# A decoder layer's first feed-forward: accumulating transfers for the residual, and a new order around its first product pairs

## The chip, the cores and the metric

The kernel runs on one core of one Trainium2 chip. The metric is device time in microseconds (us) of one launch; the figure compared is the median of several runs. The core has five engines with queues of their own: TensorE (PE, matrix products; PEld is its weight loading), VectorE (DVE), ScalarE (ACT), GpSimd (POOL) and SyncE (SP, which here only issues transfers). Each works through its instructions in order and waits on semaphores. ACT and POOL issue transfers too, in line with their other instructions.

## The reference

One decoder layer on x, 1024 tokens by 1024 channels, float32: a half-weighted feed-forward, a mixer (stick-breaking attention beside a Mamba-2 scan), a cross-attention to 256 memory tokens, and a second half-weighted feed-forward. Each part is normalised before and after. Only the first feed-forward bears on the change:

```python
f = swiglu(rmsnorm(h, ffn1_pre_g[l]), ffn1_w_gu[l], ffn1_w_down[l])
h = h + 0.5 * rmsnorm(f, ffn1_post_g[l])
m = hybrid_mixer(rmsnorm(h, mix_pre_g[l]), ...)
# swiglu(h): g, u = split(h @ w_gu); (silu(g) * u) @ w_down      inner width 2816 = 22 x 128
```

## The kernel before

Activations lie with channels on the 128 partitions and tokens along the free axis, in two halves `hh` of 512 tokens; a tile is 128 x 512. Eight tiles `d` make a half. Every operand of a product is kept as a high part (`XH`, `whi`), rounded to the format that PE takes, and a low part (`XL`, `wlo`), what rounding lost. `mm3` (L281) multiplies high by high, high by low and low by high, so a 128 x 128 block of weights against one tile is three matmuls of 512 columns. `split` (L259) makes the parts: the high one on ACT (L261), the low one on DVE (L263). Where a line of the profile reads `xl<-braw,xh` at L263, it is such a low part.

`up_phase` (L556) makes the 22 blocks `f` of gate and up. The first three (`first_seven` is 3 here) go plainly, block by block and half by half: `gate` and `up`. The other 19 go through `seven(f)` (L804), a fast scheme that makes gate and up for both halves with seven products in place of eight, each of 4 x 3 = 12 matmuls. The products' right operands are the four quarters `B11`, `B12`, `B21`, `B22` of the normalised input and three sets of sums `S`; the quarter `B12` is turned into a difference in place (`differ`, L727) and split by `last` (L717), one tile at a time, from 2.5 us after the first `seven` begins. The left operands are sums and differences of the weights' halves, made in `pieces` (L746): a 128x512 POOL instruction (L757) and a `split`. `blocks`, `ahead` and `block` hand them out in the order of the products and make up to four in advance. `prepare_all` (L234) uses the same stretch to load later weights (31 blocks, 62 steps), split them and store the parts in DRAM; a step borrows the tiles `acc0`, `acc1`, `rpost`, `dg`, `bh`, `bl`.

The down projection (`down1` L952, `down7` L992) is again seven products `m`, over 11 pairs of blocks. It needs sums of the activations of four quarters, `xs`: pairs of blocks from 4 up make them while they are at hand (`pair_sums`, L633); for the first two pairs they are loaded again, summed on DVE (L616) and stored by `act_sums` (L597), which `seven(f)` starts for f = 4 and 5. Operands of the down projection are loaded, combined (L1031) and split by `fetch`, five or more ahead.

After the products come `squares` (the sum of squares) and `post` (L380). It scales a result tile `F` by gain and norm (`apply`, L401), adds the residual tile that `resid` (L370) loaded into an `XL` tile on POOL's queue (L405), stores the new `h` (L410, POOL's queue), makes the high part for the mixer (L412, ACT) and, later, the low part (`low`, L417, DVE) and the sum of squares (`presum`, L363). For half 0 this lies beside the last products of the down projection, for half 1 beside the mixer's first projections (`ssd`).

What sets the order: PE's instructions keep the order of the program. `self.clock` adds up a planned cost of each matmul (0.422 ns a column, 216 ns for 512). Work put on `self.later` with a planned time enters the program when the clock has reached it, and is pinned behind what its engine already has (`kp`). The rest is ordered by a scheduler from data dependencies; `urgent` raises an instruction's priority. All times such as 148000, 14000 or 2600 in the code are nanoseconds on that planned clock.

Of the kernel before, what the change touches and what calls it, by code (L numbers as in the profile page):

```python
# [47 lines left out]
class Kern:  # L48
# [189 lines left out]
    def prepare_all(self, sp):  # L238
        names = [("ssd", i) for i in [*range(6), *range(12, 26)]] + [("qkv", i) for i in range(QKV)]
        pairs = [  # L240
            ((self.fp, "acc0", None), (self.fp, "acc1", None)), ((self.fp, "rpost", None), (self.tp, "dg", None)),
            ((sp, "bh", None), (sp, "bl", None)),
        ]
        raw = [(sp, "braw", 2), (sp, "braw", 2), (self.xp, "xl0", KT + 1), (self.xp, "xl1", KT + 1)]
        n = 2 * len(names)
        self.prepare(names, raw, pairs, [148000 + 3900 * i for i in range(n)])

# [131 lines left out]

    def post(self, hh, gname, r2, gnext=None, out=None, step=None, spread=True, pins=(23000, 28000), accs=None, at=None, tail=None, hold=False):  # L380


        nc = self.nc
        t1, t2 = 2500, 6000
        if accs is None:
            accs = self.new_accs()
            for d in range(KT):
                self.sumsq(accs, d, self.F[hh][d])
# [9 lines left out]
        def apply(d):  # L398
# [4 lines left out]
                )  # L403
            )
            self.kp(nc.vector.tensor_tensor(out=F, in0=F, in1=self.XL[hh][d], op=ALU.add))  # L405
            if out is not None:
                nc.sync.dma_start(out=out[d], in_=F)
                return
            self.XL[hh][d] = self.xl(hh, F32R)
            self.kp(nc.gpsimd.dma_start(out=self.h[hh][d], in_=F))  # L410
# [19 lines left out]

        def rest(d):
            low(d)
            presum(d)
# [16 lines left out]
        for d in range(KT):  # L450
            t = t3 + step * d
            q.append((t, lambda d=d: apply(d)))
            if out is None:
                q.append((t + min(step, 2600) + 300, lambda d=d: rest(d)))
        if out is None:
            t += min(step, 2600)
            c2 = self.t(self.rp, [P, 4], F32, f"cpre{hh}", bufs=2)
# [98 lines left out]
    def up_phase(self, sp, sp2, wgu, gpre, act_d, bank, load, plain, sizes, rw=None, begin=None):  # L556
# [40 lines left out]
        def act_sums(j, t0):  # L597

            x = {}
            names = ("a11", "a21", "a12", "a22")  # L600
            late = 14000 if begin else 9000

# [22 lines left out]
            for i, (n, out, a, b, op) in enumerate((  # L625
# [4 lines left out]
                at(t0 + late + 1200 * i, combine, n, out, a, b, op)  # L630
                at(t0 + late + 3000 + 1200 * i, put, n)

# [113 lines left out]
        def pieces(f):  # L746
# [3 lines left out]
            G0, G1, U0, U1 = G[:, 0:4], G[:, 4:8], U[:, 0:4], U[:, 4:8]  # L750
            for a, b, op in (
                (G0, G1, ALU.add), (U1, None, None), (G0, U1, ALU.add), (U0, G0, ALU.subtract), (G0, None, None),
                (G1, U1, ALU.subtract), (U0, U1, ALU.add),
            ):
                if b is not None:
                    t = self.t(sp if begin else sp2, [P, 4, P], F32, "wc", bufs=NWC)
                    inst = nc.gpsimd.tensor_tensor(out=t, in0=a, in1=b, op=op)  # L757
                    if begin and f == first_seven and a is G0 and b is G1:
                        self.tc.keep_in_program_order(inst)
                    a = t  # L760
# [43 lines left out]
        def seven(f):  # L804


            t5, d = (self.t(self.tp, [P, H], F32, f"sq{i}") for i in range(2))
            if later_sums and (f in (4, 5) if begin else f > 6 and f % 2):
                act_sums(later_sums.pop(0), self.clock)
# [16 lines left out]
            with self.urgent():  # L826
                nc.vector.tensor_tensor(out=e, in0=e, in1=m6, op=ALU.add)
            product(a, B12, True)
            t1 = ft()
            with self.urgent():  # L830
                scaled(t1, a, 1)
            with self.urgent():
                nc.vector.tensor_tensor(out=e, in0=e, in1=a, op=ALU.add)
            product(c, S[5], True)
# [7 lines left out]
            with self.urgent():  # L842
                nc.vector.tensor_tensor(out=e, in0=e, in1=b, op=ALU.subtract)  # L843
            nc.gpsimd.tensor_tensor(out=t1, in0=t1, in1=e, op=ALU.mult)  # L844
            if f < 4:
# [106 lines left out]
    def down1(self, sp, wdn, act_d, xs_d, gpost, gnext):  # L952
# [5 lines left out]
        accs = []  # L958
# [9 lines left out]
        def finish(m, i):  # L968
            if m == 3:
                self.run_later(float("inf"))  # L970
                for d in range(4):
                    at(5000 + 4000 * d, squares, 0, d, "acc0")
                self.resid(0, 3500, 16000)
            elif m == 4:
# [1421 lines left out]
```

## Time and profile before

| | us |
|---|---|
| median of 3 runs | 2607.29 (2604.95 to 2607.7) |
| span of the profiled execution | 2606.7 |
| PE busy | 2578.2 (99%) |
| DVE busy | 1993.9 (76%) |
| ACT busy | 1289.7 (49%) |
| POOL busy | 577.9 (22%) |

The profiled execution's own time is its span, 2606.7 us from the first instruction to the last; nothing else is recorded around it, and it lies 0.6 us under the median of the runs. All times in a trace count from the span's start. The plain blocks run up to 79 us, the `seven` pairs from 80 to 449, the down projection from there to 666, and the mixer's first projections follow. A timeline row gives start, length, engine, line, operation, `output<-inputs`, and in brackets how long the engine was idle before it and who released it. The length of a matmul reaches past the start of the next one.

### The profile page before, as it was taken

Reading aid. Unit: us, or ns where it says so; the run is one execution under the profiler, and the core shown is the slowest. Engines: PE = TensorE matmul, PEld = TensorE weight load, DVE = VectorE, ACT = ScalarE, POOL = GpSimd, SP = SyncE. Lnnn points to the kernel's source line nnn. Section 1 sums busy time; section 2 is a strip of 40 time slices with the busy share of each in tenths; the row PEclk is TensorE's granted clock in tenths of the full one; section 3 lists DMA queues with packets and bytes.
Section 4 is the critical chain, followed back from the end, with each engine's and each line's share of the span. In section 5 each row is a group of like instructions: output and inputs, shape, how many; then the busy total and the mean of one; then the engine's idle time right before and its main releaser. Section 6 shows DMA issues by size and latency. Waiting matters only on the chain.

```text
span 2606.7 us, 36814 instructions
## 1 busy us (share of the span) xinstructions
PE 2578.2 (99%) x12850; PEld 2148.5 (82%) x12850; DVE 1993.9 (76%) x3044; ACT 1289.7 (49%) x2300; POOL 577.9 (22%) x669
## 2 busy tenths in 40 slices
PE   9999999999999999999999999999999999999999
PEld 7788888888777778888888898888878888888887
DVE  7978987779689884777777777876656888777767
ACT  7434444555356663555555554445554433334543
POOL 2655554001000001111111110101011655551000
PEclk9999999999999999999999999999999999999999
DMA  6468887655656516555555556547558453326554
GB/s 241 158 210 298 300 287 272 209 188 169 224 195 204 182 69 213 162 149 152 141 152 131 169 161 215 206 153 250 196 185 299 146 183 104 109 85 236 184 174 154
DMA packets 216042, 489.82 MB, mean 188 GB/s; under 512 B 26544, under 2 KB 35120, under 8 KB 215856
## 3 DMA queue, kind: packets, MB, share of 16 engines
q1 hardware_dynamic: 169232, 381.02, 44.6%
q0 software_dynamic: 22720, 62.93, 8.1%
q10 hardware_dynamic: 23904, 43.53, 4.5%
q8 instruction: 101, 1.65, 0.3%
q14 instruction: 85, 0.70, 0.1%
HBM read 327.46 MB, written 138.94 MB: 179 GB/s over the span
## 4 chain that ended last, share of the span: by engine, by line
PE 77%; issue 13%; DVE 5%; ACT 1%; DMA 1%; POOL 0%; DVEq 0%; ACTq 0%; POOLq 0%
PE mm L139 38%; PE dn L139 34%; PE z L139 2%; PE tr L142 2%; PE ms L139 1%; PE ms L142 1%; DVE nb L1770 1%; DVE wlo L263 0%; DVE acc L363 0%; DVE hl L263 0%; DVE atl L263 0%; DVE F L1053 0%; DVE xl L263 0%; DVE F L405 0%; DVE xl L417 0%
## 5 line engine op out<-in xcount | busy, mean ns | idle before, releaser
L139 PE MATMUL mm<-xh,whi 128*128 128x512 f32 x1320 | 520.3, 403 | 2.5 <-ACT xh L268 1.1
L139 PE MATMUL mm<-xh,wlo 128*128 128x512 f32 x1272 | 488.7, 391 | 0.0
L139 PE MATMUL mm<-xl,whi 128*128 128x512 f32 (+1 forms) x1252 | 486.9, 389 | 1.8 <-DVE xl L263 1.4
L139 PEld LDWEIGHTS mm<-xh,whi 128*128 128x128 f32 x1320 | 248.2, 188 | 44.6 <-issue 3.8
L139 PEld LDWEIGHTS mm<-xh,wlo 128*128 128x128 f32 x1272 | 238.8, 188 | 52.1 <-DVE wlo L263 0.4
L139 PEld LDWEIGHTS mm<-xl,whi 128*128 128x128 f32 x1252 | 236.1, 189 | 35.9 <-DVE xl L263 2.3
L1770 DVE TENSOR_TENSOR_SCAN nb<-nb,begin 128x128 f32<-128x128 f32 (+7 forms) x128 | 171.3, 1351 | 50.8 <-ACT nb L1766 49.8
L1766 ACT ACTIVATE nb<-z,scale 128x128 f32<-128x128 f32 (+2 forms) x192 | 107.8, 581 | 78.8 <-PE z L139 78.6
L263 DVE TENSOR_TENSOR wlo<-wraw,whi 128x1024 fp32r<-128x1024 f32 x70 | 85.5, 1222 | 54.3 <-ACT whi L261 54.0
L261 ACT CAST whi<-wraw 128x1024 fp32r<-128x1024 f32 (+1 forms) x87 | 84.0, 965 | 78.3 <-PE mm L139 51.1
L658 ACT ACTIVATE ft<-ft 128x512 f32<-128x512 f32 x88 | 55.5, 631 | 99.3 <-DVE ft L657 97.3
L1787 POOL DMA_DIRECT2D mix<-sq x64 | 52.8, 826 | 231.0 <-DVE sq L1785 168.0
L139 PE MATMUL dn<-xh,wlo 128*128 128x512 f32 x296 | 101.3, 390 | 0.0
L757 POOL TENSOR_TENSOR wc<-raw,wraw 128x512 f32<-128x512 f32 x55 | 81.2, 1476 | 57.7 <-DVE blk L263 24.8
L263 DVE TENSOR_TENSOR atl<-tr,ath 128x512 fp32r<-128x512 f32 (+1 forms) x108 | 67.9, 632 | 31.2 <-ACT ath L261 30.8
L757 POOL TENSOR_TENSOR wc<-wraw,raw 128x512 f32<-128x512 f32 x56 | 80.2, 1432 | 50.9 <-DVE whi L263 16.6
L844 POOL TENSOR_TENSOR ft<-ft,e 128x512 f32<-128x512 f32 x37 | 59.7, 1614 | 121.2 <-DVE e L843 45.8
L139 PE MATMUL mm<-ath,v 128*128 128x256 f32 x320 | 85.9, 291 | 0.8 <-ACT sq L1784 0.6
L261 ACT CAST ath<-tr 128x512 fp32r<-128x512 f32 (+1 forms) x108 | 58.9, 546 | 53.3 <-PE tr L142 48.9
L139 PE MATMUL dn<-xh,blk 128*128 128x512 f32 x264 | 85.1, 389 | 0.0
L261 ACT CAST wlo<-wc 128x512 fp32r<-128x512 f32 x79 | 49.1, 621 | 69.9 <-PE dn L139 23.2
L139 PE MATMUL mm<-atl,v 128*128 128x256 f32 x320 | 82.8, 281 | 0.7 <-DVE atl L263 0.7
(579 smaller groups left out, 6775.6 us busy)
## 6 DMA issues: line engine op xcount, KB each, us to landing
whi<-dwhi SPq DMA_DIRECT2D x82, 512.0 KB, 3.6
wlo<-dwlo SPq DMA_DIRECT2D x82, 512.0 KB, 4.7
wraw<-in_w_gu SPq DMA_DIRECT2D x43, 512.0 KB, 4.0
dwhi<-bh SPq DMA_DIRECT2D x78, 256.0 KB, 4.1
dwlo<-bl SPq DMA_DIRECT2D x78, 256.0 KB, 3.9
raw<-in_w_gu SPq DMA_DIRECT2D x37, 512.0 KB, 4.0
wraw<-xs SPq DMA_DIRECT2D x56, 256.0 KB, 3.0
xs<-ft ACTq DMA_DIRECT2D x54, 256.0 KB, 3.7
```

The costliest lines, as they stand in the source:

```text
L139: self._pe(self.nc.tensor.matmul(out, lhsT, rhs, start=start, stop=stop, skip_group_check=self.more), cost)
L142: self._pe(self.nc.tensor.transpose(out, src, self.ident if ident is None else ident), 109.0)
L261: self.kp(self.nc.scalar.copy(hi, src))
L263: self.nc.vector.tensor_tensor(out=lo, in0=src, in1=hi.bitcast(F32), op=ALU.subtract)
L658: nc.scalar.activation(t, t, AF.Silu)
L757: inst = nc.gpsimd.tensor_tensor(out=t, in0=a, in1=b, op=op)
L844: nc.gpsimd.tensor_tensor(out=t1, in0=t1, in1=e, op=ALU.mult)
L1766: nc.scalar.activation(nb[:, s0:s1], z[:, 0:n], AF.Sigmoid, scale=sc[:, i : i + 1])
L1770: nc.vector.tensor_tensor_scan(out=nb[:, 0:Wd][:, ::-1], data0=nb[:, 0:Wd][:, ::-1], data1=begin[:, S - Wd : S][:, ::-1], initial=0.0, op0 ...
L1787: nc.gpsimd.dma_start(out=self.mix_d[p][a * 64 : a * 64 + 64, csl], in_=o, accum_op=ALU.add)
```

## The change

Five edits; the third also reaches the second feed-forward:

1. `post` gets a flag `fused`, which both of `down1`'s calls set. `apply` then scales `F` and issues, on POOL's queue, a transfer that adds the residual from DRAM into `F` in place (`accum_op=ALU.add`). The addition on DVE (L405) and the loads of `resid` are gone. What followed it (a new `XL` tile, the store of `h`, the high part) is a function `settle`, and is done with the low part and the sum of squares in `rest`, 6500 ns after `apply` and not 2900 (half 0) or 2300 (half 1). The closing norm's times are `tail`s of (14000, 17500) from a later base, which makes them 600 ns later for half 0 and 1200 ns later for half 1.
2. `act_sums` starts in the pairs f = 5 and 7, not 4 and 5; its sums follow 9000 ns after and not 14000, and each store 4000 ns after its sum and not 3000.
3. In the first `seven` pair the product with `B12` (`top`, with the gate that hangs on it) is the last of the seven and not the fifth; the weights come in that order.
4. The first weight sum of that pair, G0 + G1, is made by DVE and not by POOL, pinned in the program's order there.
5. `prepare_all` begins at 170000 and not 148000 on the planned clock, with steps of 3800 and not 3900.

```diff
-        self.prepare(names, raw, pairs, [148000 + 3900 * i for i in range(n)])
+        self.prepare(names, raw, pairs, [170000 + 3800 * i for i in range(n)])
...
+        res = self.h[hh]
...
+            if fused:
+                self.kp(nc.gpsimd.dma_start(out=F, in_=res[d], accum_op=ALU.add))
+                return
             self.kp(nc.vector.tensor_tensor(out=F, in0=F, in1=self.XL[hh][d], op=ALU.add))
...
+            settle(d)
+
+        def settle(d):
+            F = self.F[hh][d]
             self.XL[hh][d] = self.xl(hh, F32R)
             self.kp(nc.gpsimd.dma_start(out=self.h[hh][d], in_=F))
...
         def rest(d):
+            if fused:
+                settle(d)
             low(d)
             presum(d)
...
-                q.append((t + min(step, 2600) + 300, lambda d=d: rest(d)))
+                q.append((t + (6500 if fused else min(step, 2600) + 300), lambda d=d: rest(d)))
         if out is None:
-            t += min(step, 2600)
+            t += 6200 if fused else min(step, 2600)
...
-            late = 14000 if begin else 9000
+            late = 9000
...
-                at(t0 + late + 3000 + 1200 * i, put, n)
+                at(t0 + late + (4000 if begin else 3000) + 1200 * i, put, n)
...
-            for a, b, op in (
+            parts = [
                 (G0, G1, ALU.add), (U1, None, None), (G0, U1, ALU.add), (U0, G0, ALU.subtract), (G0, None, None),
                 (G1, U1, ALU.subtract), (U0, U1, ALU.add),
-            ):
+            ]
+            if f == first_seven:
+                parts.append(parts.pop(4))
+            for a, b, op in parts:
...
-                    inst = nc.gpsimd.tensor_tensor(out=t, in0=a, in1=b, op=op)
-                    if begin and f == first_seven and a is G0 and b is G1:
+                    early = begin and f == first_seven and b is G1
+                    inst = (nc.vector if early else nc.gpsimd).tensor_tensor(out=t, in0=a, in1=b, op=op)
+                    if early:
                         self.tc.keep_in_program_order(inst)
...
-            if later_sums and (f in (4, 5) if begin else f > 6 and f % 2):
+            if later_sums and (f in (5, 7) if begin else f > 6 and f % 2):
...
+            def top():
+                product(a, B12, True)
+                t1 = gated[1] = ft()
...
+            if f != first_seven:
+                top()
             product(c, S[5], True)
...
+            if f == first_seven:
+                top()
+            t1 = gated[1]
             nc.gpsimd.tensor_tensor(out=t1, in0=t1, in1=e, op=ALU.mult)
...
-                self.resid(0, 3500, 16000)
...
-                self.post(0, gpost, self.C[0], gnext, step=2600, accs=accs[:], tail=(17000, 20500))
+                self.post(0, gpost, self.C[0], gnext, step=2600, accs=accs[:], tail=(14000, 17500), fused=True)
...
-                self.resid(1, 2000, 14000)
...
-        self.post(1, gpost, self.C[1], gnext, step=2000, accs=accs[:], at=(6500, 9000, 10000), tail=(7500, 10500))
+        self.post(1, gpost, self.C[1], gnext, step=2000, accs=accs[:], at=(6500, 9000, 10000), tail=(4500, 7500), fused=True)
```

`up_phase` and `seven` serve both feed-forwards; `begin` tells them apart. In the second one `f == first_seven` holds for its own first pair (f = 4), so edit 3 acts there as well.

More of the change, by code (lines that the diff above doesn't have):

```diff
@@ L378, in resid, with post @@
         self.later += [(self.clock + start + step * d, lambda d=d: one(d)) for d in range(KT)]
-    def post(self, hh, gname, r2, gnext=None, out=None, step=None, spread=True, pins=(23000, 28000), accs=None, at=None, tail=None, hold=False):
+    def post(self, hh, gname, r2, gnext=None, out=None, step=None, spread=True, pins=(23000, 28000), accs=None, at=None, tail=None, hold=False, fused=False):
         nc = self.nc
         t1, t2 = 2500, 6000
+        res = self.h[hh]
         if accs is None:
@@ L827, in seven @@
                 nc.vector.tensor_tensor(out=e, in0=e, in1=m6, op=ALU.add)
[L828 to L833, printed above, removed]
+            gated = {}
+            def top():
+                product(a, B12, True)
+                t1 = gated[1] = ft()
+                with self.urgent():
+                    scaled(t1, a, 1)
+                with self.urgent():
+                    nc.vector.tensor_tensor(out=e, in0=e, in1=a, op=ALU.add)
+            if f != first_seven:
+                top()
             product(c, S[5], True)
```

## The prediction

> **What bounds the kernel now.** I read the page's head first, then TensorE's (PE's) timeline for its idle gaps up to 720 us (the first feed-forward and the start of what follows it), then the windows around each gap, then the other engines there.
>
> ```profile
> span 2606.7 us, 36814 instructions
> ...
> PE 2578.2 (99%) x12850; PEld 2148.5 (82%) x12850; DVE 1993.9 (76%) x3044; ACT 1289.7 (49%) x2300; POOL 577.9 (22%) x669
> ```
>
> PE is busy all but 28.5 us of the span, and the change takes no matmul away. So it can only win back idle time of PE, or time at a low clock. PE's timeline has four such places in the lines that the change touches (start, us, what, idle before and releaser):
>
> ```profile
> 80.27 0.50 PE L139 MATMUL mm<-xh,whi 128*128 128x512 f32 x1 [0.94 <-ACT whi L261]
> ...
> 93.90 0.50 PE L139 MATMUL mm<-xl,whi 128*128 128x512 f32 x1 [0.60 <-DVE xl L263]
> ...
> 95.70 0.50 PE L139 MATMUL mm<-xl,whi 128*128 128x512 f32 x1 [0.84 <-DVE xl L263]
> ...
> 115.10 0.39 PE L139 MATMUL dn<-xh,whi 128*128 128x512 f32 x1
> 118.48 3.72 PE L139 MATMUL mm<-S,wlo 128*128 128x512 f32 x9 [3.00 <-DVE e L823]
> ...
> 449.15 7.19 PE L139 MATMUL dn<-wlo,whi 128*128 128x512 f32 x31
> ...
> 651.38 0.73 PE L139 MATMUL dn<-hl,wlo 128*128 128x512 f32 x2 [0.76 <-DVE hl L263]
> 652.64 0.73 PE L139 MATMUL dn<-hl,dx 128*128 128x512 f32 x2 [0.52 <-ACT dx L261]
> 653.79 2.00 PE L139 MATMUL dn<-hl,dx 128*128 128x512 f32 x4 [0.42 <-DVE dx L263]
> ```
>
> The row of 449.15 is for the pace: 31 matmuls, of which one shows as 0.39 us, give (7.19 - 0.39) / 30 = 0.227 us from start to start, and a product of twelve takes 2.72. I call the places A (0.94 us, the first product of the first seven-product pair), B (0.60 + 0.84 = 1.44), C (3.00) and D (0.76 + 0.52 + 0.42 = 1.70). The windows give the clock behind C and D, and how full VectorE (DVE) is; columns are stretch, length, busy time (and instructions) of PE, PEld, DVE, ACT, POOL, then granted clock, DMA share, GB/s:
>
> ```profile
> 115.00:118.00 3.00, 0.48 (x3) 0.06 (x1) 3.00 (x4) 0.00 (x0) 1.66 (x2) 1.00 0.37 140
> 118.00:122.00 4.00, 3.52 (x9) 2.85 (x10) 4.00 (x8) 1.77 (x3) 1.09 (x1) 0.57 0.92 291
> 122.00:135.00 13.00, 13.00 (x59) 10.71 (x58) 6.24 (x10) 4.08 (x8) 9.50 (x10) 1.00 0.37 133
> ...
> 610.00:650.00 40.00, 40.00 (x182) 33.24 (x181) 39.71 (x66) 23.03 (x40) 6.49 (x13) 1.00 0.60 198
> 650.00:654.00 4.00, 2.30 (x8) 0.99 (x7) 4.00 (x8) 1.87 (x3) 1.78 (x4) 1.00 1.03 394
> 654.00:658.00 4.00, 4.00 (x11) 2.89 (x11) 2.92 (x5) 0.69 (x2) 0.30 (x1) 0.58 1.01 398
> ```
>
> After C the clock is 0.57 over 4 us, after D 0.58: 4 x 0.43 = 1.72 and 4 x 0.42 = 1.68 us more. So C costs 4.72, D 3.38, and all four 0.94 + 1.44 + 4.72 + 3.38 = 10.5 us. The brackets understate a little: 115.10 to 118.48 is 3.38 us, less the 0.23 of one matmul 3.15, not 3.00. With 0.15 more for each of the seven gaps, 11.5 us is the most there is. At C and D DVE is full (3.00 of 3.00, 39.71 of 40.00): DVE is late, not PE or a transfer.
>
> **The change, part by part.** *One weight sum on DVE (A).* The sum G0 + G1 of pair 3 is one 128x512 addition on POOL; a DVE addition beside it is stretched:
>
> ```profile
> 71.25 2.21 DVE L263 TENSOR_TENSOR xl<-bh,xh 128x512 fp32r<-128x512 f32 x1
> ...
> 76.10 2.35 DVE L730 SCALAR_TENSOR_TENSOR braw<-braw,params,braw 128x512 f32<-128x512 f32 x1
> 78.37 0.68 DVE L657 TENSOR_TENSOR ft<-mm,rpre 128x512 f32<-128x512 f32 x1
> ```
> ```profile
> 71.59 1.31 POOL L757 TENSOR_TENSOR wc<-wraw 128x512 f32<-128x512 f32 x1
> ```
> ```profile
> 79.08 0.63 ACT L658 ACTIVATE ft<-ft 128x512 f32<-128x512 f32 x1 [3.01 <-DVE ft L657]
> 79.61 1.12 ACT L261 CAST whi<-wc 128x512 fp32r<-128x512 f32 x2
> ```
>
> The chain is DVE's L657 at 78.37, ACT's L658, ACT's cast of this very sum at 79.61, PE at 80.27. Moving the sum adds 0.68 (as L657) to DVE ahead of it and takes 2.21 - 0.68 = 1.53 away: DVE is 0.85 us earlier, A shrinks by up to 0.85. If the stretch were not POOL's doing, DVE would be 0.68 later and A grow by that. Two inputs in SBUF beside a POOL sum twice stretched, and a like one not: I take the first and count 0.8 (bounds -0.7 and 0.94).
>
> The Trainium skill says the same of the cause (SBUF — State Buffer, Who interferes with whom): a DVE instruction with two SBUF inputs and a GpSimd one that reads SBUF exclude each other. By that rule A loses 0.85; by an addition's mere move it gains 0.68. The trace (2.21 beside 0.68) agrees with the rule.
>
> *The last difference used last (B).* The product with B12, whose low halves (`xl`) DVE finishes late, moves from fifth to seventh. Two products of 2.72 us take its place, so these halves have 5.4 us more.
>
> ```profile
> 90.86 0.68 DVE L263 TENSOR_TENSOR wlo<-wc,wlo 128x512 fp32r<-128x512 f32 x1
> ...
> 94.37 0.68 DVE L263 TENSOR_TENSOR blk<-wc,blk 128x512 fp32r<-128x512 f32 x1
> 94.97 0.68 DVE L263 TENSOR_TENSOR xl<-cb,xh 128x512 fp32r<-128x512 f32 x1
> ```
>
> The last `xl` is done at 95.65; its new use is after 97. Next to be late are the weights of the two products that move forward: their low halves are these rows of `wlo` (done 91.54, wanted about 92) and `blk` (done 95.05, wanted about 94.8). The second is 0.2 to 0.3 us late, and DVE comes 0.85 earlier by A. I count 1.3 of 1.44 (bounds 0.6 and 1.75). The price is at the pair's end: the gate (L657, SiLU, two VectorE steps, POOL's product) now starts after the last product. Its PSUM bank is next wanted by the fourth product of the next pair, 3 x 2.72 = 8.2 us on, so two DVE steps of 0.68 and ACT's 0.63 fit even behind a few microseconds of queue. The store is 8 us later anyway. The condition on `first_seven` holds for the second feed-forward's first pair too, where PE does not stand and DVE is full:
>
> ```profile
> 2050.00:2060.00 10.00, 9.91 (x45) 7.86 (x44) 10.00 (x14) 4.80 (x9) 7.54 (x6) 1.00 0.29 105
> ```
>
> Nothing can be won there; a weight's low half one place too late costs PE the length of one DVE step, 0.68 to 1.78 us. I count 0.3 lost (bounds 0 and 1.8).
>
> *First activations' sums later (C).* Five DVE additions (L616) leave pair 4 for pair 5; those of the second group go from pair 5 to pair 7.
>
> ```profile
> 111.48 2.38 DVE L616 TENSOR_TENSOR xl<-cb,cb 128x512 f32<-128x512 f32 x2
> ...
> 115.48 2.35 DVE L616 TENSOR_TENSOR cb<-cb,dg 128x512 f32<-128x512 f32 x2
> 117.75 0.68 DVE L823 TENSOR_TENSOR e<-sq,mm 128x512 f32<-128x512 f32 x1
> ```
>
> Four of them, 2.38 + 2.35 = 4.73 us, stand ahead of the `e` at 117.75 that C waits for. Without them `e` ends 4.7 us earlier and 3.00 is covered: all of C goes, its clock too. Their loads and stores (four and five of 256 KB, on ACT's queue) go along. Where they land, nine and not 14 us into pair 5, is about 127 to 134: DVE is busy 6.24 of 13 us there, so 4.73 fits. I count 4.6 (bounds 0 and 5.0).
>
> *Prepared weights later.* The first step of `prepare_all` goes from 148 to 170 us on the planned clock (216 ns a matmul where PE takes 227, so 1.05 us each), to clear the tile `dg` for the sums of pair 7; with 3.8 for 3.9 us a step, its last store comes 409.4 - 393.7 = 15.7, so 16.5 us, later.
>
> ```profile
> 425.44 0.38 SPq L217 DMA_DIRECT2D dwlo<-dg  x1
> ```
> ```profile
> 425.00:435.00 10.00, 10.00 (x46) 8.29 (x45) 5.83 (x10) 2.40 (x4) 1.29 (x1) 1.00 0.59 189
> 435.00:445.00 10.00, 10.00 (x46) 8.29 (x45) 5.79 (x8) 4.00 (x7) 1.29 (x1) 1.00 1.00 338
> ```
>
> The last store then falls at 442, into a stretch where the DMA engines are full, on SP's queue among the loads for the down projection, which PE begins at 449.15. Four steps of 768 KB at 338 GB/s are 9.3 us of transfers; 425 to 435 has 4.1 us free; 5.2 us move towards 449. Most of what fills 435 to 445 is loaded well ahead, so I count 0.3 us lost (bounds 0 and 5).
>
> *Residual by accumulating transfers (D).* In each `post`, eight additions L405 leave DVE; eight residual loads on POOL become eight accumulating transfers there, as many issues as before. High half, low half, sum of squares and store come 6.5 instead of 2.9 us after their `apply`.
>
> ```profile
> L405 DVE TENSOR_TENSOR F<-F,xl 128x512 f32<-128x512 f32 x8 | 5.5, 701 | 0.0
> ```
> ```profile
> 650.62 0.71 DVE L263 TENSOR_TENSOR hl<-raw,hl 128x512 fp32r<-128x512 f32 x1
> ```
>
> That group (stretch 595 to 655) is 5.5 us; back to back they come 0.60 apart, so 4.8 us of DVE. D's three gaps are 1.70 of lateness, from the `hl` of 650.62 on. So 4.8 covers it if DVE is not made to wait for the transfers. The trace has accumulating transfers of 64 KB only, and 256 KB ones that don't accumulate:
>
> ```profile
> mix<-sq POOLq DMA_DIRECT2D x64, 64.0 KB, 3.3
> xl<-h POOLq DMA_DIRECT2D x32, 256.0 KB, 4.9
> ...
> xl<-in_xT POOLq DMA_DIRECT2D x16, 256.0 KB, 7.4
> ```
>
> From 3.3 us (size makes no difference) to 4 x 3.3 = 13.2 (each byte counts). I take 5, the row of the same size, queue and direction; the 7.4 are bursts of eight. Issue to landing 5, ACT's high half 0.7: 5.7 us against 6.5 x 1.05 = 6.8. It fits, with DVE's own queue in between. Behind a waiting low half stand the operands' splits, which PE waits for; behind POOL's store stands only the next transfer. In the second `post` the sum of squares ended just in time:
>
> ```profile
> 701.46 0.68 DVE L363 TENSOR_TENSOR acc<-acc,sq 128x512 f32<-128x512 f32 x1
> ```
> ```profile
> 702.89 0.95 PE L139 MATMUL ms<-small,acc 128*128 128x1 f32 x8
> ```
>
> The `tail` sets that product 34.7 for 33.5, 1.3 us later, and DVE has 4.8 less to do; the last half is then ready near 700.5. I count 3.2 of D's 3.38 (bounds 0 and 4.4).
>
> The Trainium skill asks for no PE gap over about 3 us to keep the clock (TensorE: Matmul & The Clock Gate, Why this matters for your kernels). D's gaps are each under 1 us, and yet 0.58 stands behind them, so the trace does not agree. By the rule D would be worth 1.70 and the sum 1.7 less.
>
> **Sum.** 0.8 + 1.3 - 0.3 + 4.6 - 0.3 + 3.2 = 9.3 us, from the profiled 2606.7 to 2597.4. The median of the runs, 2607.3, is 0.6 above that execution's span: 2598.0.
>
> **Rivals.** *Half of it:* the low halves wait about as long as the additions took, and D stays. For it: DVE has no spare time from 610 to 650. Against: the 6.8 us. Gain 9.3 - 3.2 = 6.1, time 2601.
> *C only moves:* VectorE waits for the four loads in pair 5, nine us after issue where it had 14, and PE stalls as at 118. Against: 6.8 us free in that window. 9.3 - 4.6 = 4.7, time 2603.
> *Nothing is gained:* the order of the instructions shifts, and stalls of 1 us each come back elsewhere; A and B are of that size, and PE idles 28.5 - 7.1 = 21 us in other places. Time 2606.
> *Slower:* accumulating costs by the byte, 13.2 us a transfer. DVE takes eight `apply` steps in some 31 us (4.4 apart); with the halves 2.5 steps behind, each step then lasts (13.2 + 0.9) / 2.5 = 5.6 us, 1.2 x 8 = 9.9 more lateness at 650; in the second `post` the last sum is ready near 709 and PE stands 4.4 us and 1.7 at low clock. 9.9 + 6.1 - 6.1 = 9.9 slower: 2617. It decides from about 12 us a transfer. Against: 64 KB of it land in 3.3 us, most of which a larger one would not pay again.
>
> **How the numbers follow.** Forecast 0.54, half 0.14, C moves 0.10, nothing 0.12, slower 0.10. This kernel's runs tell 0.2%, 5.2 us, from no change. Faster: 0.54, most of half (0.11), a third of C moves (0.03): 0.68. Slower 0.10, same 0.22. The upper bounds of the four terms, 0.94 + 1.75 + 5.0 + 4.4 = 12.1, give 2595.2; the runs' own spread (2604.95 to 2607.7) takes the low end to 2594. The high end takes in half, C moves and most of nothing: 2606.5.
>
> **What would show it.** Right: no bracket over 0.5 us in PE's rows of 78 to 125 and 645 to 660; clock 1.00 in both stretches; DVE's L616 in pair 5; accumulating transfers landing in 4 to 6 us; no DVE wait over 1 us ahead of L417. Wrong: PE waits for DVE between 612 and 660 or at the `ms` product near 700; PE idle near 449 with SP's `xs` loads late; a bracket at the sixth product of pair 3, or between 2045 and 2062, over 0.5 us.

## The result, and the profile after

The changed kernel took 2617.08 us (median of five runs, 2616.57 to 2619.35) against 2607.29 for the kernel before: a ratio of 1.0038, 95% interval 1.0027 to 1.0049. It is slower by about 10 us, where 9 us faster was forecast. The head of the profile's page, after the change:

```profile
span 2614.8 us, 36772 instructions
...
PE 2581.4 (99%) x12850; PEld 2150.8 (82%) x12850; DVE 1980.0 (76%) x3029; ACT 1291.5 (49%) x2300; POOL 581.6 (22%) x668
```

The span is 8.1 us longer, with as many matmuls. That is less than the 9.8 us between the medians: a run's time is 1.7 to 2.2 us over its core's span, so the execution profiled before was one of some 2608.5 us, over its median, and this one took 2616.57, under its own. VectorE is busy 13.9 us less, so the work did leave it. What PE waited for stands in its timeline; these rows are in the places of A to D, at the second post and at the second feed-forward's first pair:

```profile
90.68 2.97 PE L139 MATMUL dn<-S,whi 128*128 128x512 f32 x12 [0.29 <-DVE e L837]
...
113.54 3.03 PE L139 MATMUL mm<-S,wlo 128*128 128x512 f32 x12 [0.86 <-DVE e L837]
...
626.38 0.93 PE L139 MATMUL dn<-hl,wlo 128*128 128x512 f32 x3 [2.04 <-DVE ft L1074]
...
648.71 1.23 PE L139 MATMUL dn<-hl,wlo 128*128 128x512 f32 x3 [0.73 <-ACT wlo L261]
651.29 0.92 PE L139 MATMUL dn<-hl,dx 128*128 128x512 f32 x2 [1.35 <-ACT dx L261]
...
707.03 1.86 PE L139 MATMUL ms<-small,acc 128*128 128x1 f32 x8 [4.62 <-DVE acc L363]
...
2059.60 3.01 PE L139 MATMUL dn<-S,whi 128*128 128x512 f32 x12 [3.22 <-DVE e L837]
```

A and B are gone but for 0.29 us, and of C 0.86 is left. D is worse: a new gap of 2.04 at 626, and at 648 ScalarE's casts (`wlo`, `dx`) where it had been VectorE. Two gaps more are new: 4.62 us at the sums of the second post, and 3.22 in the second feed-forward. The loss at a place can be counted as the time between matmul starts over the pace of 0.227 us. By this count PE gains 6.4 us at A to C; it loses 4.7 us more than before from 600 to 660, 6.8 at the second post and 3.1 in the second feed-forward. That is 8.2 us lost on balance, and the span grew by 8.1. The windows at two of the gaps, with the columns of the prediction's windows (the last three numbers are granted clock, DMA share and GB/s):

```profile
646.00:656.00 10.00, 7.68 (x24) 4.88 (x23) 7.24 (x13) 4.17 (x7) 0.54 (x1) 0.83 0.82 316
...
708.00:716.00 8.00, 8.00 (x32) 6.71 (x32) 1.04 (x3) 2.35 (x4) 0.00 (x0) 0.68 0.45 164
```

Both hold time at a low clock: 0.68 over the 8 us behind the second post's gap is 8 x 0.32 = 2.6 us more. And VectorE, busy 44.7 of 45 us from 610 to 655 before, is now busy 35.3: it has some 4.8 us of work less there, and stands for about as long again. Who waits for what there is in the waits of 600 to 712 us (total, times, longest):

```profile
ACT xh L420 <- DMA F<-in_xT: 24.8, 11, 3.3
...
DVE xl L425 <- ACT xh L420: 14.9, 8, 3.0
ACT xh L420 <- DMA ft<-in_xT: 10.0, 3, 8.1
```

and the times from issue to landing in the answer for line 407, the accumulating transfer:

```profile
L407 POOL DMA_DIRECT2D F<-in_xT x12: 852/857/1192, 609.0 to 693.8; - x12
L407 POOL DMA_DIRECT2D ft<-in_xT x4: 890/1062/1301, 677.9 to 680.9; - x4
...
DMA to landing us min/median/max: 3.7/7.0/11.1
```

The second half's first four result tiles are named `ft`, so these are the sixteen transfers of both halves. They take seven microseconds in the median, where 5 was taken. ScalarE stands 34.8 us at the high part `xh` (L420), waiting for landings, and VectorE 14.9 us behind ScalarE. How this reaches PE at 648 is seen in three timelines: the first half's two last issues on POOL, then ScalarE, then VectorE.

```profile
636.99 0.88 POOL L407 DMA_DIRECT2D F<-in_xT  x1 [3.50 <-DVE F L402]
...
638.92 0.86 POOL L407 DMA_DIRECT2D F<-in_xT  x1 [0.47 <-DVE F L402]
```
```profile
642.92 0.72 ACT L420 ACTIVATE xh<-F,params 128x512 fp32r<-128x512 f32 x1 [3.26 <-DMA F<-in_xT]
...
646.90 0.72 ACT L420 ACTIVATE xh<-F,params 128x512 fp32r<-128x512 f32 x1 [1.70 <-DMA F<-in_xT]
...
648.05 0.60 ACT L261 CAST wlo<-cb 128x512 fp32r<-128x512 f32 x1
```
```profile
643.68 0.75 DVE L425 SCALAR_TENSOR_TENSOR xl<-F,params,xh 128x512 fp32r<-128x512 f32 x1 [2.58 <-ACT xh L420]
...
644.95 0.68 DVE L1052 TENSOR_TENSOR cb<-xh,raw 128x512 f32<-128x512 f32 x1
```

The transfers issued at 636.99 and 638.92 are read 5.9 and 8.0 us later, as soon as they land. ScalarE came to the first reading at 642.92 - 3.26 = 639.66, 2.7 us behind the issue. VectorE, which needs that high part for the low one, stands 2.58 us for it, and so makes the sum `cb` at 644.95, ready at 645.63. The cast of that `cb` (`wlo`, 648.05) then stands behind ScalarE's second reading, which begins at 646.90, and PE's gap at 648.71 is for that cast. Landings hold up the same operand twice: its sum on VectorE, and then its cast on ScalarE.

The gap at 626 is not of that kind. PE waits there for the addition `ft` (L1074), which VectorE makes at 625.55, right behind this sum:

```profile
624.94 0.69 DVE L1052 TENSOR_TENSOR cb<-xl,wraw 128x512 f32<-128x512 f32 x1 [1.84 <-DMA wraw<-in_w_dn]
```

The sum stood 1.84 us for a weight load. Loads of this kind (`wraw<-in_w_dn`, 600 to 660 us) land 3.9 us after their issue in the median, 2.7 in the kernel before. By matmul starts over the pace PE loses 4.1 us from 600 to 632, where the kernel before loses 0.2, and 4.9 from 632 to 660, where it loses 4.2. So most of the first half's loss here stands at a late weight load, with the low clock behind it (0.72 from 626 to 632), and the smaller part at the readings above.

### The profile page after: what moved, and what is told of

Read it like the earlier page. It is cut to its first block, busy times and chain, and to the rows that moved or that the text cites. A ratio compares the mean times of both kernels' runs of the same rounds, so it can differ in the third digit from the quotient of the medians.

```text
span 2614.8 us, 36772 instructions
## 1 busy us (share of the span) xinstructions
PE 2581.4 (99%) x12850; PEld 2150.8 (82%) x12850; DVE 1980.0 (76%) x3029; ACT 1291.5 (49%) x2300; POOL 581.6 (22%) x668
## 5 line engine op out<-in xcount | busy, mean ns | idle before, releaser
L139 PE MATMUL mm<-xh,wlo 128*128 128x512 f32 x1288 | 494.7, 392 | 0.0
L263 DVE TENSOR_TENSOR atl<-tr,ath 128x512 fp32r<-128x512 f32 (+1 forms) x108 | 67.9, 632 | 31.2 <-ACT ath L261 30.9
L139 PE MATMUL dn<-xh,whi 128*128 128x512 f32 x240 | 83.2, 391 | 0.0
```

The source lines that it names most:

```text
L139: self._pe(self.nc.tensor.matmul(out, lhsT, rhs, start=start, stop=stop, skip_group_check=self.more), cost)
L263: self.nc.vector.tensor_tensor(out=lo, in0=src, in1=hi.bitcast(F32), op=ALU.subtract)
```

## The experiments

All twelve in one table; each median is of 8 to 11 runs, the ratio to the kernel before on the same chip (2607.4 to 2608.0 us). Numbers in brackets are the 95% interval; 0.001 is 2.6 us.

| kernel | median us | ratio |
|---|---|---|
| 1 no accumulating transfers | 2607.05 | 0.9998 [0.9989, 1.0007] |
| 2 as 1, new order of differences in the first feed-forward only | 2603.80 | 0.9983 [0.9975, 0.9992] |
| 3 as 2, first half accumulates | 2607.77 | 0.9998 [0.9989, 1.0007] |
| 4 as 2, second half accumulates | 2611.60 | 1.0014 [1.0005, 1.0022] |
| 5 both halves, transfers plain | 2604.12 | 0.9988 [0.9979, 0.9997] |
| 6 both halves, stores of `h` last | 2608.73 | 1.0005 [0.9996, 1.0014] |
| 7 as 3, read 5 us later | 2607.69 | 0.9999 [0.9990, 1.0008] |
| 8 as 2, steps 3.1 us apart | 2605.58 | 0.9994 [0.9985, 1.0002] |
| 9 as 2, weights prepared as before | 2604.57 | 0.9989 [0.9980, 0.9998] |
| 10 as 2, steps 3.7 us apart | 2602.26 | 0.9982 [0.9973, 0.9991] |
| 11 as 10, weights from 160 us | 2600.29 | 0.9971 [0.9960, 0.9982] |
| 12 as 10, first half accumulates, stores last | 2608.06 | 1.0001 [0.9992, 1.0010] |

**1 and 2: which edit loses.**

```diff
+                self.resid(0, 3500, 16000)
-  ... tail=(14000, 17500), fused=True)
+  ... tail=(17000, 20500))
   (and the like for the second half; in kernel 2 also:)
-            if f == first_seven:
+            if begin and f == first_seven:
```

> The changed kernel without the accumulating transfers: residual loads, VectorE additions and the old tails are back; the other four edits stay. Theory: the accumulating transfers lose 4.8 us at 610 to 660 and 7.1 at the second post against before, the others win 6.6 (8.1 less 1.5 still open) and lose 3.1 at the second feed-forward's first pair: 2607.3 - 6.6 + 3.1 = 2603.8. Rival: the sums and weights that were moved later are what crowds VectorE at 610 to 660, and the transfers are only where it shows; then gaps as in the changed kernel stay at 623 and 647 and the time stays over 2610.

> As the kernel without accumulating transfers, and the new order of the differences is confined to the first feed-forward. Theory: the 3.2 us bracket in PE's rows at the second feed-forward's first pair (the product with S[5] waiting for e = d + c) goes, and nothing else moves: 3.1 us less than the kernel without accumulating transfers, 2600.7. Rival: the stall there is VectorE's full load in that pair and comes with the longer queue of the moved work, not with the order; then the bracket stays and the time is the same within 1 us.

Without the accumulating transfers the 10 us are gone (1.0038 to 0.9998). With the order confined to the first feed-forward another 3.25 us go, as expected, and the bracket at the second feed-forward with them. Both lie 3 us over what was expected. A little under half of that is in kernel 2's trace, a gap at 472 that takes 1.4 us from one matmul's start to the next over the pace, and that neither the kernel before nor the changed one has (its row begins behind the gap):

```profile
474.38 5.76 PE L139 MATMUL dn<-hl,dx 128*128 128x512 f32 x24 [1.20 <-ACT F L1106]
```

**3 and 4: one half at a time.** Kernel 3 takes kernel 2 and gives back `fused=True` with its tail to the first half, kernel 4 to the second.

> As the kernel with the order confined to the first feed-forward, and accumulating transfers for the first half's post alone (half the rows, in the middle of the down projection); the second half has its loads and additions. Theory (a wait on each transfer's round trip that ScalarE and VectorE cannot pass, each post by itself): the loss of 4.8 us at 610 to 660 is here, none at 700: 2600.7 + 4.8 = 2605.5. Rival (the first half's lateness is handed on to the second post): the gap at 702 shows here too, over 2 us, and the time is 2608 or more.

> The counterpart of the run with accumulating transfers in the first half alone: here only the second half's post has them, the first half keeps loads and additions, and the order of the differences is confined to the first feed-forward. Theory (each post loses by itself): the gap of 5 us and the half clock at 702 are here, 610 to 660 is as without such transfers: 2603.8 + 7.1 = 2610.9. The loss of both halves together would then be 4.0 (measured for the first) + 7.1 = 11.1, and the changed kernel less its 3.25 at the second feed-forward is 2613.8, 10.0 over 2603.8. Rival (the 702 gap is lateness handed on from the first half): without fused work ahead of it the second post has under 2 us of gap, 2605 or less.

Against kernel 2 the first half costs 4.0 us (4.8 expected), the second 7.8 (7.1 expected): the two posts lose each for itself, and by its trace and its median the second is the dearer one. By the intervals each figure is good to some 3 us, so their sum of 11.8 does not contradict the 10.0 that both halves together cost by the estimate under experiment 5. Kernel 4's trace has the second post's gap without any fused work ahead of it:

```profile
704.20 1.86 PE L139 MATMUL ms<-small,acc 128*128 128x1 f32 x8 [4.71 <-DVE acc L363]
```

**5: the same transfers without accumulating.**

```diff
-                self.kp(nc.gpsimd.dma_start(out=F, in_=res[d], accum_op=ALU.add))
+                self.kp(nc.gpsimd.dma_start(out=F, in_=res[d]))
```

> The changed kernel with the order confined to the first feed-forward (2613.8 by the two runs before), and the sixteen transfers no longer accumulate: a plain transfer of the same 256 KB from the same place to the same tile, so the scaled feed-forward is overwritten and left out of the result. Issues, waits and places stay. Theory A (the cost is the accumulating: 128 packets of 2048 B at 178 ns, 1.4 us of all 16 DMA engines for a transfer, where the plain ones of 4096 B take 0.64): landings fall from 7 to 4 or 5 us, the gaps at 623, 647 and 702 shrink by over half, 2604 to 2608. Theory B (any round trip through memory is too long for the 6.8 us and for what is queued behind it in order): landings 5 to 7, gaps stay, 2611 to 2614.

It took 2604.1 us, as theory A says. The changed kernel with the order confined was not run; by kernels 1 and 2 it is some 2613.8 us, so accumulating itself costs 9 to 10 us. Landing fell from 3.7/7.0/11.1 to this, and the second post's gap is gone:

```profile
DMA to landing us min/median/max: 3.0/5.0/7.1
```
```profile
699.09 0.95 PE L139 MATMUL ms<-small,acc 128*128 128x1 f32 x8
```

The first post's does not vanish: PE loses 6.0 us at 600 to 660 (time between matmul starts over the pace) where kernel 2 loses 5.1 and kernel 3 9.5. All it loses over kernel 2 lies before 632, at sums that wait for weight loads, as at 626 in the changed kernel. ScalarE still stands 27.2 us at the readings of both halves, and the kernel is as fast as kernel 2: how long ScalarE stands is no measure of the loss. What counts is what stands behind a reading, and whether PE wants it then.

Five microseconds in the median is the value the prediction had taken, from rows of plain transfers. What accumulating does to the DMA engines is seen where the second post's first four transfers run, in windows of 5 us (queue, packets, MB, share of 16 engines). First the changed kernel, 681 to 686, then the plain one, 677 to 682:

```profile
q0 software_dynamic: 339, 0.63, 71.8%
q1 hardware_dynamic: 68, 0.21, 14.6%
```
```profile
q0 software_dynamic: 320, 1.05, 55.1%
q1 hardware_dynamic: 207, 0.76, 45.9%
```

Accumulating, 0.63 MB take 0.718 x 5 = 3.6 us of all sixteen engines, 5.7 us a MB; plain, 1.05 MB take 2.8, or 2.6 a MB. The packets are half as large: from 600 to 660 us, where both kernels send 4.20 MB on q0, the changed one does it in 1792 packets and 30.9% of the engines' time, the plain one in 1280 and 19.1%, which is 64 packets and 0.9 us of all engines more for each of the eight transfers. One transfer of 256 KB thus holds all engines for 1.5 us and not 0.7, and the weight loads beside it (q1) had 14.6% of them in the one window and 45.9% in the other.

**6: the stores behind the transfers.**

```diff
-            self.kp(nc.gpsimd.dma_start(out=self.h[hh][d], in_=F))
...
+            self.later.append((max(self.clock, T0 + t3 + step * 7) + 6600 + 100 * d, put))
```

> The changed kernel with the order confined to the first feed-forward (2613.8), and the eight stores of the sum that follow the accumulating transfers on GpSimd's queue are issued together behind the last of them, in both posts. Theory A (a store that waits for its landing holds up the next accumulating transfer in GpSimd's order): GpSimd's waits at the store ahead of a transfer go, landings count from earlier, the 702 gap falls from 5 to 3 us or less, 2609 to 2611. Theory B (the DMA engines and the landing itself set the time, GpSimd has slack): within 1.5 us of 2613.8.

It took 2608.7 us, under even theory A's 2609 to 2611. POOL stands 5.4 us at its stores, where it was 19.5, and the second post's gap shrank from 4.62 us to this:

```profile
702.33 1.05 PE L139 MATMUL ms<-small,acc 128*128 128x1 f32 x8 [0.97 <-DVE acc L363]
```

But that gap did not shrink by the cause that theory A names. POOL issues the last transfer at 692.87 where the changed kernel does at 693.75, 0.9 us earlier, and waits for VectorE's `apply` before it in both. First the changed kernel's POOL and ScalarE, then the same two of kernel 6 (its line 426 is line 420):

```profile
693.75 0.86 POOL L407 DMA_DIRECT2D F<-in_xT  x1 [0.50 <-DVE F L402]
```
```profile
704.87 0.72 ACT L420 ACTIVATE xh<-F,params 128x512 fp32r<-128x512 f32 x1 [1.15 <-DMA F<-in_xT]
```
```profile
692.87 0.86 POOL L407 DMA_DIRECT2D F<-in_xT  x1 [1.08 <-DVE F L402]
```
```profile
700.16 0.72 ACT L426 ACTIVATE xh<-F,params 128x512 fp32r<-128x512 f32 x1 [1.36 <-DMA F<-in_xT]
```

From issue to use it is 11.1 us there and 7.3 here. With the stores issued between the transfers, the last transfer lands 3.8 us later although it is issued about as early: it is the transfers' own way that is longer, not POOL's order. That they wait behind the stores in the queue they share fits; the trace does not show packets' order by transfer, so it is argued.

**7 and 12: more distance, or more time, for the first half.** Kernel 7 reads 11.5 us after `apply` and not 6.5; kernel 12 spreads the steps to 3.7 us and has the stores last.

```diff
-                q.append((t + (6500 if fused else ...
+                q.append((t + (11500 if fused else ...
   (kernel 12 instead:)
-                self.post(0, ..., step=2600, accs=accs[:], tail=(14000, 17500), fused=True)
+                self.post(0, ..., step=3700, accs=accs[:], tail=(5700, 9200), fused=True)
```

> As the kernel with accumulating transfers in the first half alone, but what reads a transfer's result comes 11.5 in place of 6.5 us behind the step that issues it (planned clock, 12.1 us of PE's pace), and the last sums are planned for the same time as in the kernel changed. Theory (the transfers' landing of 7 to 11 us is longer than the 6.8 us left for it, and ScalarE stands in order behind it): the waits of ScalarE and VectorE on landings fall from 24.8 and 10.0 to a few us, the gaps at 623 and 647 go, and so does VectorE's late work of before at 651: 2600.7 - 3.4 = 2597.3. Rival (the transfers take DMA engines' time from the weight loads, and that is the loss): the gaps stay wherever the reading is put, 2604 to 2606.

> As the kernel with the steps 3.7 us apart (2602.3), but the first half's residual by accumulating transfers, 6.5 us planned from step to reading, with its eight stores behind them all; the second half has loads and additions. Theory (an accumulating transfer costs some 2 us more to land than a plain one and DMA time of the weight loads beside it, and VectorE's lateness shortens the planned distance): VectorE has 4.8 us less to do, so its steps keep their times, but ScalarE still waits at several readings; PE loses 2 to 4 us more at 610 to 655 than without: 2604 to 2606. Rival (with the steps wide enough apart the transfers are hidden and VectorE's 4.8 us are won): PE's gaps of 646 to 648 go, 2600.

Both theories were too kind. Kernel 7 is no faster than kernel 3, and kernel 12 loses 5.8 us to its twin without accumulating (kernel 10). In kernel 7 ScalarE's waits for the accumulating transfers did fall, to 6.9 us from kernel 3's 17.2, but PE's gaps from 644 to 652 stayed (0.21, 1.85 and 1.35 us, where kernel 3 has 2.06 and 1.05), as its rival says. VectorE loses at the start what it was to save, to late weight loads, and by 640 ScalarE waits for a landing again:

```profile
615.82 0.69 DVE L1053 TENSOR_TENSOR cb<-xl,wraw 128x512 f32<-128x512 f32 x1 [2.56 <-DMA wraw<-in_w_dn]
```
```profile
643.09 0.72 ACT L420 ACTIVATE xh<-F,params 128x512 fp32r<-128x512 f32 x1 [3.49 <-DMA F<-in_xT]
```

Kernel 12 is the sharper case. Its landings are shorter, 5.5 us, and still ScalarE waits 23.5 us for those of the one half. In kernel 12 the landings, the wait, a late issue on POOL, ScalarE's order, VectorE's, and PE's gap:

```profile
DMA to landing us min/median/max: 3.9/5.5/6.8
```
```profile
ACT xh L426 <- DMA F<-in_xT: 23.5, 7, 5.5
```
```profile
645.00 0.86 POOL L407 DMA_DIRECT2D F<-in_xT  x1 [7.00 <-DVE F L402]
```
```profile
649.39 0.72 ACT L426 ACTIVATE xh<-F,params 128x512 fp32r<-128x512 f32 x1 [3.42 <-DMA F<-in_xT]
...
650.54 0.60 ACT L261 CAST dx<-cb 128x512 fp32r<-128x512 f32 x1
```
```profile
641.49 0.75 DVE L431 SCALAR_TENSOR_TENSOR xl<-F,params,xh 128x512 fp32r<-128x512 f32 x1 [2.84 <-ACT xh L426]
...
648.36 0.68 DVE L1059 TENSOR_TENSOR cb<-xh,raw 128x512 f32<-128x512 f32 x1
```
```profile
651.19 1.65 PE L139 MATMUL dn<-hl,dx 128*128 128x512 f32 x3 [3.47 <-ACT dx L261]
```

The seventh transfer is issued at 645.00; ScalarE is at its reading at 649.39 - 3.42 = 645.97, 1.0 us later, where 6.8 had been planned, and stands there until 649.39. The landing of 4.4 us would have fitted into 6.8. So in the first half it is not the landing alone: the 6.5 us are between planned times, POOL waits for an `apply` that VectorE runs late, and ScalarE, with less to do, comes to the reading in time and holds the casts behind it. PE's 3.47 us are for such a cast, of the sum that VectorE has ready at 649.04: 1.5 us of them are the stand behind the reading, and the rest is VectorE's lateness, which had itself stood 2.84 us behind an earlier reading.

**8 and 10: VectorE's lateness at D, without accumulating.** Kernel 8 only changes the step, kernel 10 also the second half's first squares (17000 to 20000).

```diff
-                self.post(0, gpost, self.C[0], gnext, step=2600, accs=accs[:], tail=(17000, 20500))
+                self.post(0, gpost, self.C[0], gnext, step=3100, accs=accs[:], tail=(13500, 17000))
   (kernel 10: step=3700, tail=(9300, 12800))
```

> No accumulating transfers; the order confined to the first feed-forward (2603.8); the eight steps of the first half's post are planned 3.1 in place of 2.6 us apart, and the last sums stay planned for the same time. Theory (at 645 to 651 VectorE is late because 41 us are packed full by a spacing that is closer than needed: the last sum of squares is done at 646 and wanted at 655): the operand splits come ahead of the post's last steps, the gaps of 1.36 + 0.52 + 0.42 us and the half clock behind them go, 5.1 us, 2599. Rival (VectorE's whole load to 656 is what is late, in any order): the gaps move to the sums at 655 and the time stays within 1.5 us of 2603.8.

> No accumulating transfers, the order confined to the first feed-forward (2603.8); the eight steps of the first half's post are planned 3.7 in place of 2.6 us apart with its last sums for the same time, and the second half's first squares 3 us later. Theory (VectorE's work that is wanted before 645 is too much only because the post's steps are among it; at 3.1 the last steps still stood ahead of the splits): two steps of 2.6 us move behind 650, the gaps of 645 to 650 shrink by over half, 3 to 5 us less: 2600. Rival (the loads of the down projection or ScalarE's casts are as late as VectorE): the gaps stay, 2603 to 2606.

At 3.1 us nothing is gained. At 3.7 the trace loses 2.2 us at 600 to 660 where kernel 2 loses 5.1 (time between matmul starts over the pace), but the times, 2602.3 and 2603.8, do not tell the two apart.

**9 and 11: the prepared weights.** Kernel 9 puts `prepare_all` back to 148000 and 3900, kernel 11 starts it at 160000.

> No accumulating transfers, the order confined to the first feed-forward (2603.8), and the prepared weights back at their planned times of before (from 148 us, 3.9 apart). Theory (storing them some 16 us later fills the DMA engines at 445 to 455, the loads of the down projection are late, and PE's new gap of 1.2 to 1.9 us at 472 is theirs): the gap goes, DMA share of 445 to 455 back from 1.04 to about 0.75, 1.5 us less: 2602.3. Rival (the gap at 472 is ScalarE's order of casts and evictions there and has nothing to do with the stores): gap and time stay, 2603.8, or more if the sums of pair 7 now wait for the tile that the prepared weights share with them.

> The kernel with the steps 3.7 us apart and no accumulating transfers (2602.3), with the prepared weights planned from 160 in place of 170 us. Theory: the gap of 1.3 us at 472 (late weight stores) goes; the sums of pair 7, which cost 2.4 us when the weights were planned from 148, have their tile in time: 2600.9. Rival: the 2.4 us come back as well, 2603.

Kernel 9 has no gap at 472, and the DMA share of 445 to 455 fell from 1.04 to 0.74; but PE has two new gaps, of 0.76 us at 190 and 1.05 at 211, in the stretch where the prepared weights and the second group of `act_sums` now both use the tile `dg`. Kernel 2's window, kernel 9's, and the second of the gaps:

```profile
445.00:455.00 10.00, 10.00 (x46) 8.28 (x45) 6.71 (x11) 4.83 (x9) 3.73 (x6) 1.00 1.04 390
```
```profile
445.00:455.00 10.00, 10.00 (x46) 8.29 (x45) 7.29 (x12) 5.27 (x10) 3.93 (x6) 1.00 0.74 247
```
```profile
211.26 2.11 PE L139 MATMUL dn<-S,whi 128*128 128x512 f32 x8 [1.05 <-DVE e L837]
```

That the shared tile is what makes `e` late there is not shown: the `e` of the second gap, at 210.52, waits 1.18 us for POOL's difference (L832). From 160 us neither shows: kernel 11 has the lowest median of all, 2600.3 us, 0.9971 [0.9960, 0.9982] of the kernel before, though its interval overlaps kernel 10's. It has edits 2, 3 (in the first feed-forward), 4 and 5 (from 160 us), kernel 10's steps and squares, and no accumulating transfers. Of D a bracket of 0.85 us at 646.10 is left, at full clock.

## Why the prediction was wrong, step by step

**A, one weight sum on VectorE: right in what it won, its working in part.** The bracket at 80 is gone. VectorE's rows there:

```profile
69.27 1.95 DVE L263 TENSOR_TENSOR xl<-bl,xh 128x512 fp32r<-128x512 f32 x1
...
71.81 0.68 DVE L771 TENSOR_TENSOR wc<-wraw 128x512 f32<-128x512 f32 x1
...
73.01 0.68 DVE L263 TENSOR_TENSOR xl<-bh,xh 128x512 fp32r<-128x512 f32 x1
```

The sum's neighbour `xl<-bh,xh`, 2.21 before, takes 0.68 too, so the stretch came with POOL's sum, as taken. But POOL's next sum comes earlier now, at 69.35, and another low half beside it takes 1.95. So of the 1.53 us that VectorE was to be spared, 1.27 come back. The gate's first step (L657, now L667) starts at 75.54 and not 78.37, ahead of the long difference that stood before it; that this order closes A is argued.

**B, the last difference last: right in the first feed-forward** (0.29 of 1.44 us left, 1.3 counted), **wrong in the second.** The price counted was for "a weight's low half one place too late", and that was not what came late. The third product's bank must be read by `e = d + c` (L837) before S[5] accumulates into it; with `top` moved behind, one product of 2.72 us lies between and not two. I counted the deadlines of the operands that move forward, and not that of the result whose bank is written again sooner. Price 3.25 us where 0.3 stood, outside the bounds of 0 and 1.8.

**C, first sums later: right, a little small.** The stall fell from 3.00 us and 1.72 of clock to 0.86 us at full clock, 3.9 us of 4.6. What is late next is POOL's difference of the first two products (L832):

```profile
112.80 0.69 DVE L837 TENSOR_TENSOR e<-sq,mm 128x512 f32<-128x512 f32 x1 [1.19 <-POOL sq L832]
```

**Prepared weights: mis-sized.** 0.3 counted, bounds 0 and 5. It is 0 in the changed kernel and 1.3 to 1.9 us in kernels 1, 2, 4 and 10 (0.4 in kernel 8). The gap takes both the late weights and the loads of the first half's residual: it is in no kernel without these loads, nor in kernels 9 and 11, which prepare the weights earlier.

**D, the residual by accumulating transfers: the step that failed.** It read: 5 us of landing, "5.7 us against 6.5 x 1.05 = 6.8. It fits, with DVE's own queue in between." Four things were wrong in it. The 5 us were of plain transfers; accumulating makes 7.0 of them and twice the DMA time, shown by kernel 5. The 6.8 us were between planned times and shrank to 2.7 in the changed kernel and 1.0 in kernel 12, where VectorE's `apply` was late; kernel 12's landings would have fitted. I asked what stands behind VectorE's low half and POOL's store, and not behind ScalarE's high part, where the casts of the weights stand, and VectorE's own low half again. And the weight loads beside the transfers were left out, though most of the first half's loss in the changed kernel stands at one of them (4.1 us from 600 to 632, where it was 0.2). With plain transfers it is 1.2 there, so accumulating makes most of it; that it does so by taking the DMA engines' time from these loads is argued. The 3.2 us counted as won became 4.0 lost (kernel 3). That VectorE loses 4.8 us of work was right, but it stood waiting for as long.

**The second post: the same 5 us of landing, a second time.** "The last half is then ready near 700.5", it read. The last transfer, issued at 693.75, was read only at 704.87, 11.1 us later. PE stood 4.62 us and then ran at a low clock: 7.8 us lost (kernel 4), counted at nothing. With plain transfers the gap is gone (kernel 5).

**The rivals.** "Slower" had 2617 and 0.10, and 2617.1 came out. Its terms were not those measured: no transfer took the 13.2 us from which it decides, and the first half lost 4 and not 9.9 us. Its second post, 4.4 us and 1.7 of clock, was the right place at about the right price; the second feed-forward's 3.25, which it lacks, made up part of the rest. That it fits to 0.1 us is chance. The prediction's own signs of being wrong did show: PE waited between 612 and 660, at the `ms` product near 700, and between 2045 and 2062.

The sum in kernel 2's edits, without D and the second feed-forward, was 6.4 us (0.8 + 1.3 + 4.6 - 0.3): 2600.9. Kernel 2 gives 3.6 us (2607.4 to 2603.8). Of the 2.8 us missing, C is 0.7 and the gap at 472 is 1.1 (1.4, of which 0.3 was counted). At 600 to 660 kernel 2's trace loses 0.8 more than the kernel before; but its execution took 2606.07 us, 2.3 over its median, so the last part stays open.

## What to carry to other kernels

A transfer put in place of an instruction is read by an engine that works in order: ask what stands behind that reading on each engine, and count the distance from when the issuing engine really gets there, not from the plan. Price an accumulating transfer by a row of an accumulating one of like size, or by its DMA time as well as its landing. When products change places, look at when the banks of their results are written again, besides when their operands are ready.

## What was not expected of the hardware

An accumulating transfer of 256 KB from DRAM into SBUF took 5.7 us of all sixteen DMA engines a MB against 2.6 plain (the windows of kernel 5's section), its issue 0.86 us on POOL against 0.54, and 7.0 us to land against 5.0.

Low clock does not follow the size of the gaps alone. In the kernel before, brackets of 0.76, 0.52 and 0.42 us at D are followed by a clock of 0.58 over 4 us. Kernel 9 has the same three, the first a little longer, and keeps full clock, and so does kernel 4 with 1.22, 0.52 and 0.42 (kernel 9's PE rows, then its window of 646 to 656):

```profile
647.62 0.73 PE L139 MATMUL dn<-hl,wlo 128*128 128x512 f32 x2 [0.83 <-DVE hl L263]
648.88 0.73 PE L139 MATMUL dn<-hl,dx 128*128 128x512 f32 x2 [0.52 <-ACT dx L261]
650.03 1.71 PE L139 MATMUL dn<-hl,dx 128*128 128x512 f32 x4 [0.42 <-DVE dx L263]
```
```profile
646.00:656.00 10.00, 8.12 (x36) 5.50 (x35) 8.53 (x15) 3.89 (x7) 2.34 (x5) 1.00 1.01 384
```

The Trainium skill (TensorE: Matmul & The Clock Gate, Why this matters for your kernels) asks for no idle gap of PE over about 3 us between bursts of matmuls, to avoid a drop in throughput. By that rule none of these gaps would cost the clock: kernels 4 and 9 agree, the kernel before does not. What decides between them stays open. A term for the low clock is then a chance and not a sum, and 1.7 us of C's and of D's price in the prediction were such terms.
